# Two gated products per head group moved from VectorE to GpSimd, and earlier writes of a head's reciprocals, in an attention layer

## The chip, the cores and the metric

The kernel runs on one core of one Trainium2 chip. The metric is the device time of one execution in microseconds (us). A core has TensorE (PE in the profile; PEld is its weight load), VectorE (DVE), ScalarE (ACT), GpSimd (POOL) and SyncE (SP). Each engine has its own instruction stream, executed in order; SP and POOL here also issue the DMAs.

## The reference, cut to what matters

The program is a two-layer encoder on 512 tokens with 16 learned meta tokens in front (528 columns), model width 2048: layer 0 is softmax attention, layer 1 gated linear attention. The change lies in layer 0, whose end is

```python
q_blocks = ...                       # 16 heads in 8 groups of 2, one k/v head per group
o = softmax(q k^T / sqrt(128)) v     # per head
return (o * silu(gate)) @ w_out      # gate: a projection as wide as o
```

So each head has a 128 x 528 output `o`, a division by the softmax sums, and a product with `silu(gate)`.

## The kernel before, in words

All matrix products are made in three passes over high and low parts of their operands (`split`: the high part is a copy on ACT, line 131, the low part a subtraction on DVE, line 132). Before the attention groups, gates of heads 0 to 12 are projected and stored in a scratch tensor `g_d` (so "stored gates").

Then one loop goes over `KV` = 8 groups. In group g TensorE does, interleaved: the attention of the two heads of group g, and the projections of k and the two q of group g+1 (`qkv`). After a projection, `rotate` exchanges rows by four DMAs (line 313) and does three products and sums on POOL (lines 314 to 316); line 334 on DVE multiplies by the norm, and the result is split into the next group's q or k.

The attention of a group has nine items: four 128-query tiles of its first head, one item with the 16 meta queries of both heads (index 8), and four tiles of the second head. For each, `softmax` writes scores to the one PSUM tile `s` (TensorE, lines 685 to 687), takes the row maximum `mx` (DVE, line 690), the exponential `pn` (ACT, line 693), and a reciprocal of the sum into a column of `rs` (DVE, line 699). Because `s` has one buffer, the next item's scores can start only when `pn` has been made. Half a slot later `transposed` makes the transposes `pT` (line 705), and their parts `ph` and `pl` (lines 709 and 710), and `weighted` multiplies them by v into `o`, which is copied to `o_sb` (line 730). The first head's `o_sb` is whole soon after item 8.

The outputs are not divided at once. The reciprocals are columns of a small tile and are needed as a row over all partitions, so `inverses` writes them to a scratch tensor `r_d` (SP, lines 645 and 648) and `inverse` reads them back with a broadcast (POOL, line 637). `stored_gates` handles the two heads of the group before: it loads the stored gates into `gr` (POOL, line 654), multiplies by the row norm (DVE, line 658), makes `silu` (ACT, lines 139 to 141; POOL, line 673), calls `inverse`, and then for each head `divided` (POOL, lines 641 and 642) turns `gs` into gate over sum; DVE multiplies `o_sb` by it (line 666), and POOL issues the store to `og_d` (line 667). `gr` and `gs` have two buffers each. Head 13's gate is projected in the last group and handled in the loop itself (line 797).

The order on each engine: the program is written as generators driven by a clock of TensorE's work, where `yield 3.0` says that the next step is to come 3 us later. That gives each instruction its place in the program and with it a priority; weights get a higher one. The compiler's list scheduler then makes each engine's stream by these priorities and by its own estimates of when operands are ready, so an instruction whose operands are expected early can stand well before its place in the program. At run time the streams are fixed, and an instruction that waits holds up all behind it on its engine.

In the stage before, `first_group` normalises group 0's k and q beside the projections. It splits the squares, waits 4.4 us by the clock, and sums them with two matrix products (lines 536 and 537).

Of the kernel before, what the change touches and what calls it, by code (L numbers as in the profile page):

```python
# [14 lines left out]
ALU = mybir.AluOpType  # L15
# [7 lines left out]
SEQ = 512  # L23
META = 16
# [58 lines left out]
def hybrid_encoder(  # L83
# [5 lines left out]
    nc = tc.nc  # L89
    V, A, G, PE = nc.vector, nc.scalar, nc.gpsimd, nc.tensor  # L90
# [12 lines left out]
    og_d = scratch.tile([KT, P, T], F32, name="og_d")  # L103
    h1_d = scratch.tile([4, P, D], F32, name="h1_d")
    g_d = scratch.tile([21, P, T], F32, name="g_d")
    r_d = scratch.tile([KV, 2, T], F32, name="r_d")
# [14 lines left out]
    def col(i):  # L121
        return cols[:, i:i + 1]
# [7 lines left out]
    def split(hi, lo, src):  # L130
        A.copy(hi, src)  # L131
        V.tensor_tensor(lo, src, hi.bitcast(F32), op=ALU.subtract)  # L132

    def rsqrt_inplace(t):
        A.activation(t, t, AF.Ln)
        A.activation(t, t, AF.Exp, scale=-0.5)
# [173 lines left out]
    def rotate(qw, qs):  # L310
        for b in range(4):
            s = b ^ 1
            nc.gpsimd.dma_start(out=qs[b * 32:b * 32 + 32, :], in_=qw[s * 32:s * 32 + 32, :])  # L313
        G.tensor_tensor(qw, qw, cos, op=ALU.mult)
        G.tensor_tensor(qs, qs, sin, op=ALU.mult)
        G.tensor_tensor(qw, qw, qs, op=ALU.add)
# [207 lines left out]
    def first_group():  # L524

        for qw, w in zip(qws, (KN, QN, QN)):
            sq = fr.tile([P, T], F32, tag="sq", name="sq")
            A.activation(sq, qw, AF.Square)
            A.activation(qw, qw, AF.Copy, scale=col(w))
            for a, b in HALVES:  # L530
                parts = fr.tile([P, 2, HALF], F32R, tag="qs", name="shl")
                sh, sl = parts[:, 0], parts[:, 1]
                split(sh, sl, sq[:, a:b])
                yield 4.4
                ps = ps_t.tile([P, 512], F32, tag="t", name="ssq")[:, :HALF]
                PE.matmul(ps, ones_r, sh, start=True, stop=False)
                PE.matmul(ps, ones_r, sl, start=False, stop=True)
                V.scalar_tensor_tensor(sq[:, a:b], ps, 1.0 / P, erow[:, a:b], op0=ALU.mult, op1=ALU.add)
                yield 0.2
            rotate(qw, fr.tile([P, T], F32, tag="qs", name="qs"))  # L540
            rsqrt_inplace(sq)
            yield 9.4
            V.tensor_tensor(qw, qw, sq, op=ALU.mult)
            yield 0.4
# [82 lines left out]
    def qkv(g):  # L627
        qk, outs = qks[g % 2]
        vv = values(g)
        for i, c in enumerate((2048 + g * P, 2 * g * P, (2 * g + 1) * P)):  # L630
            qw, sq, evac = take(col(KN if i == 0 else QN))
            project(w_in0, c, HALVES, evac)
            rope(qw, sq, outs[i], (4.0, 8.8, 9.8))
        return qk, vv

    def inverse(h, rb):
        nc.gpsimd.dma_start(out=rb, in_=r_d[h // 2, h % 2:h % 2 + 1, :].broadcast_to([P, T]))

    def divided(gs, rb):
        by = gs[:, :SEQ].rearrange("p (t q) -> p t q", t=4)  # L640
        G.tensor_tensor(by, by, rb[:, :SEQ].rearrange("p (q t) -> p t q", t=4), op=ALU.mult)
        G.tensor_tensor(gs[:, SEQ:], gs[:, SEQ:], rb[:, SEQ:], op=ALU.mult)

    def inverses(g, rs):
        nc.sync.dma_start(out=r_d[g, :, :SEQ].rearrange("a (p t) -> p a t", t=4),
                          in_=rs[:, :8].rearrange("p (a t) -> p a t", a=2))
        for a in range(2):
            nc.sync.dma_start(out=r_d[g, a, SEQ:].unsqueeze(1), in_=rs[a * META:(a + 1) * META, 8:9])

    def stored_gates(hs, held):  # L650

        grs = [wa.tile([P, T], F32, tag="gr", name="gr") for _ in hs]
        for gr, h in zip(grs, hs):
            nc.gpsimd.dma_start(out=gr, in_=g_d[h])
        yield 8.0
        gss = []
        for gr, h in zip(grs, hs):
            V.tensor_tensor(gr, gr, rrow, op=ALU.mult)
            gss.append(silu(gr))
            inverse(h, gr)  # L660
            yield 5.0
        for gr, gs, h in zip(grs, gss, hs):
            divided(gs, gr)
            yield 3.0
            og = held[h % 2]
            V.tensor_tensor(og, og, gs, op=ALU.mult)
            nc.gpsimd.dma_start(out=og_d[h], in_=og)
            yield 2.0

    def silu(gr):  # L670
        gs = wa.tile([P, T], F32, tag="gs", name="gs", bufs=2)
        sigmoid(gs, gr)
        G.tensor_tensor(gs, gs, gr, op=ALU.mult)
        return gs

    def gate(h, last_k=None):
        gr = wa.tile([P, T], F32, tag="gr", name="gr", bufs=2)
        project(w_in0, 4096 + h * P, HALVES,
                lambda ps, a, b: V.tensor_tensor(gr[:, a:b], ps, rrow[:, a:b], op=ALU.mult), last_k)
        return silu(gr)  # L680
# [33 lines left out]
    def p_tiles():  # L714
        ph = wa.tile([P, 4, 272], F32R, tag="ph", name="ph")
        pl = wa.tile([P, 4, 272], F32R, tag="pl", name="pl")
        pmt = wa.tile([REP, 272], F32R, tag="pmt", name="pmt")
        return ph, pl, pmt
# [18 lines left out]
    def attention(g, qk, vv, o_sb, slot):  # L737
        qh, ql, kh, kl = qk
        q0 = (0, Q1)
        last = g == KV - 1  # L740
        rs = None if last else wa.tile([P, 9], F32, tag="rs", name="rs")
        early, late = [[[None], [None]] for _ in range(2)]

        def tile_of(a, t):
            cell, end = (late, 272) if t > 1 else (early, 256)
            t2 = t % 2
            done = t2 and not (t > 1 and a == 0)
            return (P, q0[a] + t * P, [(cell[a], 0, t2 * P, P)], [(cell[a], 256 * (t > 1), end, a)] if done else [],
                    [] if t2 else [cell[a]], a * 4 + t)
        todo = [tile_of(0, t) for t in range(4)]  # L750
        todo.append((2 * META, SEQ, [(late[a], a * META, 256, META) for a in range(2)], [(late[0], 256, 272, 0)],
                     [late[1]], 8))
        first = tile_of(1, 2)
        todo += [first[:4] + ([],) + first[5:], tile_of(1, 3), tile_of(1, 0), tile_of(1, 1)]
        prev = None
        for item in todo + [None]:
            if item is not None:
                n, c, puts, ends, fresh, i = item
                pn = softmax(n, qh[:, c:c + n], ql[:, c:c + n], kh, kl, None if last else rs[:, i:i + 1])
            yield slot / 2  # L760
            if prev is not None:
                n_, _, puts_, ends_, fresh_, _ = prev[0]
                for cell in fresh_:
                    cell[0] = p_tiles()
                transposed(prev[1], n_, [(cell[0], qc, cc, m) for cell, qc, cc, m in puts_])
                for cell, cc, m, a in ends_:
                    clk.after(slot * 1.1, lambda cell=cell, cc=cc, m=m, a=a:
                              weighted(cell[0], cc, m, vv, o_sb[a], last))
            yield slot / 2
            prev = (item, pn) if item is not None else None  # L770
        if not last:
            inverses(g, rs)
        yield slot * 0.65 if last else 0.0

    def o_tiles():
        return [wa.tile([P, T], F32, tag="o", name="o_sb", bufs=4) for _ in range(2)]

    qk, vv = qks[0][0], values(0)
    held = None
    for g in range(KV):  # L780
        o_sb = o_tiles()
        if g == KV - 1:
            clk.after(10.5, make_sel)
        att = clk.drive(chain(iter([3.0]), attention(g, qk, vv, o_sb, SLOTS[g])))
        gates = [] if g == 0 else [2 * g - 2, 2 * g - 1]
        stored = clk.drive(stored_gates([h for h in gates if h < 13], held))
        if g + 1 < KV:
            nxt = qkv(g + 1)
        for h in gates:
            if h < 13:  # L790
                continue
            gs = gate(h)
            rb = wa.tile([P, T], F32, tag="gr", name="rb")
            inverse(h, rb)
            divided(gs, rb)
            og = held[h % 2]
            V.tensor_tensor(og, og, gs, op=ALU.mult)
            nc.gpsimd.dma_start(out=og_d[h], in_=og)
        if g + 1 < KV:
            clk.finish(att, stored)  # L800
            qk, vv = nxt
            held = o_sb
# [266 lines left out]
    for a, b in HALVES:  # L1069
        ps = ps_t.tile([P, 512], F32, tag="t", name="lrf")[:64, :b - a]  # L1070
        PE.matmul(ps, fold, lt[:, a:b], start=True, stop=True)
        for d in range(2):
            pd, t = ps[d * 32:d * 32 + 16], lrs[d]
# [83 lines left out]
    gs = cg.tile([P, 4, SEQ], F32, name="gs")  # L1157
# [395 lines left out]
```

## Time and profile before

| | |
|---|---|
| median of 3 runs | 1807.34 us (1804.43 to 1808.29) |
| profiled execution, its own time | 1808.31 us |
| its span (first to last instruction) | 1806.5 us |
| mean granted TensorE clock | 0.993 of full |
| attention groups | about 286 to 790 us of the span |
| PE busy | 1750.5 us (97%) |
| DVE busy | 1148.5 us (64%) |
| ACT busy | 1005.5 us (56%) |
| POOL busy | 361.8 us (20%) |

Times in rows are us from the start of the span. A row of the timeline gives start, duration, engine, line, operation and tiles; in brackets stand the engine's idle time just before it and what ended it. A row of the waits gives who waited for whom, the total in us, how often, and the longest. In rows of stretches "PEclk" is the granted TensorE clock as a share of full speed.

### The profile page before, as it was taken

To read this page: it belongs to the slowest core of one execution; us is meant where nothing else is said; L and a number is where in the kernel's file an instruction comes from. 1 tells how busy PE (TensorE), PEld (TensorE's weight loads), DVE (VectorE), ACT (ScalarE), POOL (GpSimd) and SP (SyncE) were. 2 spreads that over 40 slices of the span, in tenths; PEclk is the share of its full clock that TensorE was granted. 3 is DMA by queue.
4 is the path that set the end of the run, shared out by engine and by line. 5 is a ranking of instruction groups with operands and counts; after the bars stand their busy time and mean duration, and the time that the engine had idled before them with its cause. 6 is when DMAs were issued, how large, how long until landed. Compare 5 with 4: busy or idle time off the path is not lost. (4 is left out here: it accounts for less than half of the span.)

```text
span 1806.5 us, 31569 instructions
## 1 busy us (share of the span) xinstructions
PE 1750.5 (97%) x12427; PEld 1641.0 (91%) x12427; DVE 1148.5 (64%) x1805; ACT 1005.5 (56%) x2056; POOL 361.8 (20%) x478
## 2 busy tenths in 40 slices
PE   8999999999999899899999999999999999999998
PEld 8999999998998889899999999988898988888886
DVE  5868765565556555596758776658585865764224
ACT  5635446566656655564547545468585765853221
POOL 3114102434543442232232101110010100000000
PEclk9999999999999999899999999999999999999999
DMA  8444434324322433264476444343342332354323
GB/s 257 141 123 125 131 116 124 96 80 116 103 84 80 111 99 104 71 214 124 130 221 190 121 134 126 95 124 102 86 113 75 114 92 76 99 157 175 94 93 128
DMA packets 272276, 218.81 MB, mean 121 GB/s; under 512 B 13084, under 2 KB 243168, under 8 KB 271600
## 3 DMA queue, kind: packets, MB, share of 16 engines
q1 hardware_dynamic: 253088, 157.41, 30.7%
q0 software_dynamic: 19040, 59.40, 10.0%
q8 instruction: 97, 1.59, 0.4%
q14 instruction: 51, 0.42, 0.1%
HBM read 176.83 MB, written 33.44 MB: 116 GB/s over the span
## 5 line engine op out<-in xcount | busy, mean ns | idle before, releaser
L154 PE MATMUL pp<-uh,whi 128*128 128x264 f32 (+1 forms) x1872 | 587.1, 314 | 1.1 <-POOL whi L383 1.0
L156 PE MATMUL pp<-uh,wlo 128*128 128x264 f32 (+1 forms) x1872 | 577.5, 309 | 1.5 <-DVE wlo L132 1.2
L155 PE MATMUL pp<-ul,whi 128*128 128x264 f32 (+1 forms) x1872 | 578.1, 309 | 0.8 <-DVE ul L445 0.8
L132 DVE TENSOR_TENSOR wlo<-wraw,whi 128x1024 fp32r<-128x1024 f32 (+1 forms) x226 | 275.9, 1222 | 236.3 <-ACT whi L131 231.5
L131 ACT CAST whi<-wraw 128x1024 fp32r<-128x1024 f32 (+1 forms) x226 | 235.2, 1041 | 258.3 <-PE f L1465 83.4
L156 PEld LDWEIGHTS pp<-uh,wlo 128*128 128x128 f32 x1872 | 355.1, 190 | 18.9 <-DVE wlo L132 1.6
L154 PEld LDWEIGHTS pp<-uh,whi 128*128 128x128 f32 x1872 | 355.4, 190 | 17.3 <-POOL whi L383 1.3
L155 PEld LDWEIGHTS pp<-ul,whi 128*128 128x128 f32 x1872 | 355.8, 190 | 14.6 <-DVE ul L445 1.3
L131 ACT CAST whi<-x 128x1024 fp32r<-128x1024 f32 x72 | 75.6, 1050 | 111.6 <-PE pp L241 51.7
L132 DVE TENSOR_TENSOR wlo<-x,whi 128x1024 fp32r<-128x1024 f32 x72 | 93.4, 1302 | 41.7 <-ACT whi L131 41.5
L693 ACT ACTIVATE pn<-s,mx 128x528 f32<-128x528 f32 (+1 forms) x72 | 50.2, 698 | 62.5 <-DVE mx L690 62.4
L240 PE MATMUL px<-uh,whi 128*128 128x264 f32 x288 | 82.2, 285 | 1.2 <-ACT whi L131 1.2
L242 PE MATMUL px<-uh,wlo 128*128 128x264 f32 x288 | 82.1, 285 | 1.0 <-DVE wlo L132 1.0
L241 PE MATMUL px<-ul,whi 128*128 128x264 f32 x288 | 81.5, 283 | 0.0
L1465 PE MATMUL f<-whi,ul 128*128 128x512 f32 x192 | 75.6, 394 | 0.0
L1463 PE MATMUL f<-whi,uh 128*128 128x512 f32 x192 | 75.5, 393 | 0.0
L1464 PE MATMUL f<-wlo,uh 128*128 128x512 f32 x192 | 75.3, 392 | 0.0
L313 POOL DMA_DIRECT2D qs<-qw x96 | 48.1, 506 | 108.1 <-ACT sq L307 70.4
L690 DVE TENSOR_REDUCE mx<-s 128x1 f32<-128x528 f32 (+1 forms) x72 | 50.7, 704 | 29.0 <-PE s L687 28.4
L710 DVE TENSOR_TENSOR pl<-pT,ph 128x512 fp32r<-128x512 f32 (+1 forms) x80 | 47.7, 596 | 25.6 <-ACT ph L709 25.0
L685 PE MATMUL s<-kh,qh 128*128 128x264 f32 (+1 forms) x144 | 43.5, 302 | 19.2 <-ACT pn L693 19.2
L242 PE MATMUL pp<-t0h,wlo 128*128 128x264 f32 x192 | 54.5, 284 | 1.2 <-DVE wlo L132 1.2
(488 smaller groups left out, 4429.7 us busy)
## 6 DMA issues: line engine op xcount, KB each, us to landing
wraw<-in_gla_w_in_dram SPq DMA_DIRECT2D x82, 512.0 KB, 3.9
wraw<-in_attn_w_in_dram SPq DMA_DIRECT2D x75, 512.0 KB, 4.3
wraw<-in_gla_w_out_dram SPq DMA_DIRECT2D x32, 512.0 KB, 3.9
wraw<-in_attn_w_out_dram SPq DMA_DIRECT2D x23, 512.0 KB, 4.4
x<-in_attn_w_in_dram SPq DMA_DIRECT2D x19, 512.0 KB, 4.1
x<-in_gla_w_in_dram SPq DMA_DIRECT2D x14, 512.0 KB, 4.8
qs<-qw POOLq DMA_DIRECT2D x96, 66.0 KB, 4.4
g_d<-y POOLq DMA_DIRECT2D x20, 264.0 KB, 2.4
```

Source lines behind the costliest of these rows:

```text
L131: A.copy(hi, src)
L132: V.tensor_tensor(lo, src, hi.bitcast(F32), op=ALU.subtract)
L154: PE.matmul(ps, wh, uh[:, k, a:b], start=first, stop=False)
L155: PE.matmul(ps, wh, ul[:, k, a:b], start=False, stop=False)
L156: PE.matmul(ps, wl, uh[:, k, a:b], start=False, stop=last)
L240: PE.matmul(ps, w[0][:, k], bh[:, k], start=k == 0 and not more, stop=False, skip_group_check=more)
L241: PE.matmul(ps, w[0][:, k], bl[:, k], start=False, stop=False, skip_group_check=more)
L242: PE.matmul(ps, w[1][:, k], bh[:, k], start=False, stop=k == KH - 1, skip_group_check=more)
L690: V.reduce_max(mx, s, axis=AX.XY, negate=True)
L1463: PE.matmul(ps, uh[:, k, ts], wh[:, kk], start=(k == 0), stop=False)
L1464: PE.matmul(ps, uh[:, k, ts], wl[:, kk], start=False, stop=False)
L1465: PE.matmul(ps, ul[:, k, ts], wh[:, kk], start=False, stop=(k == KT - 1))
```

## The change

Three edits, all in layer 0.

1. In `first_group` the pause between the splits and the sums is 5.6 instead of 4.4 us.
2. `inverses` writes one head at a time. The first head's reciprocals are written in mid group, once item 8's softmax has been issued; the second head's at the end, half a slot earlier than before. A head takes two DMAs on SP; a group took three before and takes four now.
3. The product of `o_sb` with the divided gate is on POOL, directly behind the division, and its store directly behind it, for the 13 stored gates and for head 13.

```diff
@@ first_group
                 split(sh, sl, sq[:, a:b])
-                yield 4.4
+                yield 5.6
@@
-    def inverses(g, rs):
-        nc.sync.dma_start(out=r_d[g, :, :SEQ].rearrange("a (p t) -> p a t", t=4),
-                          in_=rs[:, :8].rearrange("p (a t) -> p a t", a=2))
-        for a in range(2):
-            nc.sync.dma_start(out=r_d[g, a, SEQ:].unsqueeze(1), in_=rs[a * META:(a + 1) * META, 8:9])
+    def inverses(g, rs, a):
+        nc.sync.dma_start(out=r_d[g, a, :SEQ].rearrange("(p t) -> p t", t=4), in_=rs[:, a * 4:a * 4 + 4])
+        nc.sync.dma_start(out=r_d[g, a, SEQ:].unsqueeze(1), in_=rs[a * META:(a + 1) * META, 8:9])
@@ stored_gates
             divided(gs, gr)
+            og = held[h % 2]
+            G.tensor_tensor(og, og, gs, op=ALU.mult)
+            nc.gpsimd.dma_start(out=og_d[h], in_=og)
             yield 3.0
-            og = held[h % 2]
-            V.tensor_tensor(og, og, gs, op=ALU.mult)
-            nc.gpsimd.dma_start(out=og_d[h], in_=og)
-            yield 2.0
@@ attention
             yield slot / 2
+            if not last and (item is None or item[5] == 8):
+                inverses(g, rs, item is None)
             if prev is not None:
...
             prev = (item, pn) if item is not None else None
-        if not last:
-            inverses(g, rs)
@@ the loop over groups, head 13
-            V.tensor_tensor(og, og, gs, op=ALU.mult)
+            G.tensor_tensor(og, og, gs, op=ALU.mult)
```

## The prediction

> **What bounds the kernel now.** I began with the stretches of the span, to see where TensorE is idle.
>
> ```profile
> span 1806.5 us, 31569 instructions
> 286.00:790.00 504.00, 472.19 (x3743) 459.01 (x3743) 297.89 (x569) 308.08 (x750) 200.34 (x245) 0.98 0.36 101
> 790.00:1807.00 1017.00, 1000.57 (x6464) 908.16 (x6463) 648.65 (x1001) 557.46 (x1087) 108.32 (x157) 1.00 0.42 124
> ```
>
> The first number after the length is PE's busy time. TensorE is the bound throughout, but in the attention stage it is idle for 504.0 - 472.2 = 31.8 us, twice as long as in the thousand us behind it, and its granted clock (the third number from the end) is 0.98 there. DVE works for 298 of 504 us there, so it is not full. Next, the waits of PE and of DVE in that stage:
>
> ```profile
> PE s L685 <- ACT pn L693: 19.2, 8, 3.7
> PE pT L705 <- DVE pl L710: 4.3, 5, 1.7
> PE sums L733 <- DVE pl L710: 2.0, 1, 2.0
> ...
> DVE o_sb L666 <- POOL gs L642: 45.8, 13, 7.5
> DVE gr L658 <- DMA gr<-g_d: 15.6, 13, 1.9
> DVE o_sb L797 <- POOL gs L642: 2.2, 1, 2.2
> ```
>
> 19.2 us of PE's idle time are scores that wait for the exponential. The timeline of group 1's start, then of groups 4, 6 and 7, shows what makes it late:
>
> ```profile
> 349.92 0.71 DVE L666 TENSOR_TENSOR o_sb<-o_sb,gs 128x528 f32<-128x528 f32 x1 [2.97 <-POOL gs L642]
> 353.25 1.50 DVE L658 TENSOR_TENSOR gr<-gr,rrow 128x528 f32<-128x528 f32 x1 [0.97 <-DMA gr<-g_d]
> 357.82 0.71 DVE L666 TENSOR_TENSOR o_sb<-o_sb,gs 128x528 f32<-128x528 f32 x1 [2.73 <-POOL gs L642]
> 358.44 0.70 DVE L690 TENSOR_REDUCE mx<-s 128x1 f32<-128x528 f32 x1
> 359.18 0.70 ACT L693 ACTIVATE pn<-s,mx 128x528 f32<-128x528 f32 x1 [1.56 <-DVE mx L690]
> 360.02 0.59 PE L685 MATMUL s<-kh,qh 128*128 128x264 f32 x1 [2.04 <-ACT pn L693]
> 361.21 0.71 DVE L658 TENSOR_TENSOR gr<-gr,rrow 128x528 f32<-128x528 f32 x1 [1.46 <-DMA gr<-g_d]
> ...
> 535.96 0.71 DVE L666 TENSOR_TENSOR o_sb<-o_sb,gs 128x528 f32<-128x528 f32 x1 [5.42 <-POOL gs L642]
> 538.16 0.39 PE L685 MATMUL s<-kh,qh 128*128 128x264 f32 x1 [1.55 <-ACT pn L693]
> 668.71 0.39 PE L685 MATMUL s<-kh,qh 128*128 128x264 f32 x1 [3.01 <-ACT pn L693]
> 723.96 0.71 DVE L666 TENSOR_TENSOR o_sb<-o_sb,gs 128x528 f32<-128x528 f32 x1 [7.50 <-POOL gs L642]
> 726.16 0.59 PE L685 MATMUL s<-kh,qh 128*128 128x264 f32 x1 [3.73 <-ACT pn L693]
> 729.58 0.71 DVE L334 TENSOR_TENSOR qw<-qw,sq 128x528 f32<-128x528 f32 x1 [2.60 <-POOL qw L316]
> ```
>
> The gated product stands in DVE's stream in front of a row maximum and waits for POOL's division; maximum, exponential and the next scores follow one behind the other, and TensorE stops. The pairs at 536 and 724 give the slack: 5.42 - 1.55 = 3.9 and 7.50 - 3.73 = 3.8. A single wait of DVE below about 3.8 us costs TensorE nothing (the one at 349.92 left no gap); a second wait in the same slot costs nearly all of itself (2.73 gave 2.04).
>
> The stretches after five of these stops, of which the first and the last two are shown with the sum of all, have a second price:
>
> ```profile
> 360.40:363.30 2.90, 2.90 (x15) 2.90 (x15) 2.08 (x4) 2.87 (x8) 0.57 (x1) 0.50 0.27 109
> ...
> 726.20:731.00 4.80, 4.80 (x22) 4.80 (x23) 2.13 (x6) 2.13 (x6) 3.80 (x4) 0.50 0.16 54
> 745.50:749.00 3.50, 3.50 (x18) 3.50 (x17) 1.53 (x4) 1.52 (x5) 0.00 (x0) 0.51 0.00 0
> sum 17.50, PE 17.48 PEld 17.48 DVE 10.07 ACT 12.73 POOL 5.98; mean PE 3.50 PEld 3.50 DVE 2.01 ACT 2.55 POOL 1.20
> ```
>
> For 17.5 us in all TensorE had a clock of 0.50 to 0.53: about 17.5 x 0.49 = 8.6 us lost.
>
> **The change, part by part.** The base is the profiled execution's 1808.3 us (span 1806.5 and 1.8 around it), 1.0 above the median.
>
> *Product to POOL.* The nearest rows for its parts:
>
> ```profile
> L666 DVE TENSOR_TENSOR o_sb<-o_sb,gs x13: 707/709/710, 349.9 to 724.0; 128x528 f32<-128x528 f32 x13
> L673 POOL TENSOR_TENSOR gs<-gs,gr x16: 1316/1323/1336, 298.7 to 780.9; 128x528 f32<-128x528 f32 x16
> L667 POOL DMA_DIRECT2D og_d<-o_sb x13: 547/587/590, 354.1 to 725.0; - x13
> ```
>
> DVE loses 14 x 0.71 = 9.9 us of work and, what counts, the 45.8 + 2.2 us in which it waited for POOL. POOL gains 14 x 1.32 = 18.5 us; it is busy for 200 of 504. In its own stream the product needs no signal from another engine beyond `o_sb`, and the store follows it as it did. What goes from the path: the scores' waits 19.2, the transposes' waits 4.3 (each follows a slot that DVE began late), the `sums` wait 2.0 (DVE's `pl` stood behind head 13's product), and the half clock 8.6: 34.1 us.
>
> *What DVE waits for next.* It no longer stops for POOL's lateness, so it meets it at line 658, whose gate load (POOL, line 654) is issued only when the division has freed `gr`. Of these 13 waits 11 come behind a division. At a group's start the lateness is the 2.97 + 0.97 = 3.9 us of the first two rows of the timeline, and up to 1.32 + 0.59 = 1.9 more if the product and its store are issued ahead of the load. Against a slack of 3.8 this is 0.1 to 2.0 us of TensorE each, 1 to 22 in all. I take 0.4, near the lower end, since that pair of waits, the nearest row, left no gap and the second pair, which cost 2.04, goes to another place: 11 x 0.4 = +4.4.
>
> *Reciprocals in mid group.* Rows of group 0:
>
> ```profile
> 316.54 0.79 SPq L648 DMA_DIRECT2D r_d<-rs  x2
> 339.55 0.57 SPq L645 DMA_DIRECT2D r_d<-rs  x1
> 325.42 2.01 POOL L313 DMA_DIRECT2D qs<-qw  x4 [9.45 <-ACT sq L307]
> 329.56 0.39 ACT L730 COPY o_sb<-o 128x272 f32<-128x272 f32 x1 [0.87 <-PE o L728]
> 333.25 1.33 POOL L316 TENSOR_TENSOR qw<-qw,qs 128x528 f32<-128x528 f32 x1
> 341.11 0.71 DVE L334 TENSOR_TENSOR qw<-qw,sq 128x528 f32<-128x528 f32 x1 [0.43 <-issue]
> 343.53 0.59 POOL L637 DMA_DIRECT2D gr<-r_d  x1 [8.95 <-DMA r_d<-rs]
> 348.17 1.54 POOL L641 TENSOR_TENSOR gs<-gs,gr 128x512 f32<-128x512 f32 x1 [1.52 <-DMA gr<-r_d]
> ```
>
> Both small writes already leave at item 8, because their operands are ready; now the first head's large one can leave with them at about 316.5. With the 4.0 us from 339.55 to 343.53 and the 4.6 from there to 348.17, its division comes at about 325 instead of behind the boundary, and its product after the copy at 329.56. So one of the two chains that collide at each boundary moves to a quieter place: this is why I expect one wait per slot and not two. On SP there are seven more DMAs of under 0.6 us, 4 us at most; they stand where line 648 stood, wait for no later reciprocal, and only weight loads are behind them: 0. On POOL the rotation is behind the division and product: 1.76 + 1.32 + 0.59 = 3.7 us later in mid group, covered because line 316 ends at 334.6 and line 334 starts at 341.1, 6.5 later; without that cover it would be the excess over 6.5. At the boundary the last rotation gets 1.9 us more in front but loses one broadcast and one division: 0, with +1 as upper bound each (7 in all).
>
> *POOL against DVE.* The row at 353.25 took 1.50 us, the same work at 361.21 took 0.71: the first ran beside a product of POOL. A product on POOL can then hold a DVE product of two SBUF operands by 0.8 us; 14 of them are 0 to 11 us of DVE, within the slack: 0.
> [...]
>
> *The pause of 5.6.* The rows of the earlier stage:
>
> ```profile
> PE ssq L537 <- DVE shl L132: 1.2, 2, 0.6
> L537 PE MATMUL ssq<-shl,ones_r x6: 279/283/391, 122.2 to 172.6; 128*128 128x264 f32 x6
> ```
>
> A gain of 0 to 1.2; the six pauses push the chain out by 7.2 us, and after 172.6 there are over 100 us of cover until 286. I take 0, as the wait may pass to another row.
>
> **Sum:** 1808.3 - 34.1 + 4.4 = 1778.6, say 1779.
>
> **The rivals.**
> (a) *The wait moves to line 658.* If product and store stand before the gate load, the upper bound above holds: +22 instead of +4.4, so 1796. For it: POOL's stream puts what is first in the program first. Against: the load needs only the division's end.
> (b) *The early write brings nothing*, because the first head's chain still runs at the boundary. Then two waits per slot stay and about half the 34.1 goes: 1791. Against: both small writes did leave at 316.54.
> (c) *Slower: POOL's rotation becomes the bound.* Line 334 would wait for line 316, with the next group's q and the row maximum behind it. To undo 34.1 us, each of seven boundaries must cost 4.9, so the rotation must be late by 3.8 + 4.9 = 8.7 us; at 10 us the time is 1808.3 - 34.1 + 7 x 6.2 = 1818. For it: at the last boundary line 334 waited 2.6 for POOL. Against: only 3.7 us are put in front of it.
> (d) *The half clock is not due to these stops*, apart from the longest. Then 12.7 x 0.49 = 6.2 us stay: 1785. Against: five stretches, each right behind a stop of about 2 us or more; for it: a stop of 3.0 at 668.7 had none.
> [...]
> (e) *POOL holds DVE* for the whole 11 us on the path: 1790.
>
> **How the numbers follow.** Main case 0.55 (own range 1773 to 1788), (a) 0.18, (b) 0.09, (c) 0.06, (d) 0.05, (e) 0.04, nothing measurable (a pile-up of several of these terms) 0.03. The lower end is the 34.1 with no new wait and the pause's gain, and some us for other DVE work that comes earlier: 1770; the upper end takes in (a), (b), (e) and some room: 1801. 0.2% (3.6 us) is about what a measurement of this kernel tells from no change: faster 0.88, same 0.05, slower 0.07.
>
> **What would show it.** Right: line 666 is gone from DVE's waits and nothing of 45 us takes its place; the scores' wait for `pn` is under 6 us; no stretch at half clock in the groups; line 637 and the first division of each group lie in mid group. Wrong: DVE's wait at line 658 grows from 15.6 beyond 40 us (a), or line 334 waits for POOL by more than 3.8 us at each boundary (c), or the clock stays at 0.98 in the stage although the stops are gone (d).

## The result, and the profile after

The changed kernel takes 1799.52 us (median of 5 runs, 1796.92 to 1800.92) against 1808.29 for the kernel before, a ratio of 0.9953 (95%: 0.9939 to 0.9968). It is 8.8 us faster where 29 were forecast. Its profiled execution took 1799.52 us too.

In the changed kernel the lines behind the edit have moved up by two or three: the row norm is line 656 (it was 658), the gate load 652 (654), the gated product on POOL 663 and its store 664 (666 and 667), the row maximum 687 (690), the exponential 690 (693), the scores 682 (685), the transposes 702 (705), `pl` 707 (710).

Span, and two stretches (as before: PE's busy time is the number after the length, its clock the third from the end); the second stretch is the only one at half clock behind a stop in the attention groups:

```profile
span 1797.5 us, 31585 instructions
286.00:790.00 504.00, 478.82 (x3855) 465.55 (x3854) 308.63 (x573) 315.82 (x757) 227.37 (x262) 1.00 0.40 108
364.50:367.10 2.60, 2.60 (x14) 2.60 (x13) 2.54 (x6) 1.66 (x5) 0.00 (x0) 0.51 0.12 28
```

PE is idle for 504.0 - 478.8 = 25.2 us of the same 504, where it was 31.8, and the clock is 1.00 instead of 0.98. The waits in that window show what was exchanged:

```profile
PE s L682 <- ACT pn L690: 12.8, 6, 3.0
PE pT L702 <- DVE pl L707: 6.0, 12, 0.7
...
DVE gr L656 <- DMA gr<-g_d: 28.9, 9, 5.3
DVE qw L334 <- POOL qw L316: 7.7, 2, 4.8
```

DVE's 45.8 us at the product are gone, and the wait for the gate load has grown from 15.6 to 28.9. The scores still wait for 12.8 us where 19.2 stood, now once at each of six boundaries. Where the stage begins and ends is told by its groups of scores and of output casts, here after (first and last start stand behind the three durations):

```profile
L682 PE MATMUL s<-kh,qh x144: 280/284/422, 293.1 to 755.3; 128*128 128x264 f32 x128, 128*32 128x264 f32 x16
L131 ACT CAST uh<-o_sb x2: 636/642/647, 771.1 to 774.9; 128x528 fp32r<-128x528 f32 x2
```

Before, the first scores started at 290.5 and the last cast of an output at 786.6. From the one to the other the stage takes 481.8 us instead of 496.1: 14.3 gained. Ahead of it 2.6 are lost (290.5 to 293.1), and behind it 2.7. The program behind it is unchanged, and in the seventeen profiles of this study that part took 1019.6 to 1023.3 us (1026.2 in one), so this loss is not put down to the change. The sum, -14.3 + 2.6 + 2.7 = -9.0, is the difference of the spans.

The timeline of the changed kernel: the first rows are the early write, the mid-group division and the next gate's row norm in group 0, then come the boundary to group 1, the boundary at 541 on DVE, ACT and PE, and the end of the last of six boundaries with a stop.

```profile
312.10 0.34 SPq L645 DMA_DIRECT2D r_d<-rs  x1
324.18 1.56 POOL L641 TENSOR_TENSOR gs<-gs,gr 128x512 f32<-128x512 f32 x1 [3.14 <-DMA gr<-r_d]
330.38 0.69 DVE L656 TENSOR_TENSOR gr<-gr,rrow 128x528 f32<-128x528 f32 x1
...
341.89 0.57 SPq L645 DMA_DIRECT2D r_d<-rs  x1
345.61 0.58 POOL L637 DMA_DIRECT2D gr<-r_d  x1 [5.72 <-DMA r_d<-rs]
350.92 1.54 POOL L641 TENSOR_TENSOR gs<-gs,gr 128x512 f32<-128x512 f32 x1 [2.49 <-DMA gr<-r_d]
352.72 1.32 POOL L663 TENSOR_TENSOR o_sb<-o_sb,gs 128x528 f32<-128x528 f32 x1
353.99 0.59 POOL L652 DMA_DIRECT2D gr<-g_d  x1
354.57 0.55 POOL L664 DMA_DIRECT2D og_d<-o_sb  x1
358.20 1.51 DVE L656 TENSOR_TENSOR gr<-gr,rrow 128x528 f32<-128x528 f32 x1 [4.96 <-DMA gr<-g_d]
363.31 0.39 PE L682 MATMUL s<-kh,qh 128*128 128x264 f32 x1 [3.00 <-ACT pn L690]
...
541.55 0.93 DVE L656 TENSOR_TENSOR gr<-gr,rrow 128x528 f32<-128x528 f32 x1 [5.33 <-DMA gr<-g_d]
542.57 0.65 ACT L139 ACTIVATE gs<-gr 128x528 f32<-128x528 f32 x1 [4.78 <-DVE gr L656]
542.75 0.69 DVE L687 TENSOR_REDUCE mx<-s 128x1 f32<-128x528 f32 x1
543.12 0.63 ACT L135 ACTIVATE sq<-sq 128x528 f32<-128x528 f32 x1
543.65 0.63 ACT L140 ACTIVATE gs<-gs 128x528 f32<-128x528 f32 x1
544.19 0.63 ACT L136 ACTIVATE sq<-sq 128x528 f32<-128x528 f32 x1
544.72 0.63 ACT L141 ACTIVATE gs<-gs 128x528 f32<-128x528 f32 x1
545.25 0.68 ACT L690 ACTIVATE pn<-s,mx 128x528 f32<-128x528 f32 x1
546.08 0.39 PE L682 MATMUL s<-kh,qh 128*128 128x264 f32 x1 [2.84 <-ACT pn L690]
...
664.20 0.71 DVE L334 TENSOR_TENSOR qw<-qw,sq 128x528 f32<-128x528 f32 x1 [4.82 <-POOL qw L316]
666.40 0.39 PE L682 MATMUL s<-kh,qh 128*128 128x264 f32 x1 [1.50 <-ACT pn L690]
```

The first head of group 0 went as forecast: its division comes at 324.18, and the gate loaded into the freed buffer (330.38) costs DVE no wait. At the boundary the second head's reciprocals leave at 341.89, come back as a broadcast that POOL can use at 350.92, 9.0 us later, and behind division and product, but ahead of the product's store, the gate load is issued at 353.99. DVE waits 4.96 us for it, then TensorE 3.00.

The boundary at 541 shows why the slack was not 3.8. The row maximum ends at 542.75 + 0.69 = 543.44, and the exponential starts only at 545.25: on ACT five activations stand in front of it, three of the silu that the waiting gate has just released (139 to 141) and two of the next group's norm (135 and 136). In the kernel before, the same step went from 359.14 to 359.18. The same five stand there at each of the five boundaries where DVE waits for the load. DVE's wait and TensorE's stop were 4.96 and 3.00, 4.30 and 1.66, 5.06 and 2.43, 5.33 and 2.84, 3.98 and 1.40: a slack of 2.5 to 2.6, and of 2.0 at the first boundary, where the row norm itself took 1.51. The lateness was forecast at 3.9 us and up to 1.9 more; it came to between 4.0 and 5.3. At the last of the six stops, DVE waits for POOL's rotation (664.20) instead, at 1.50 of TensorE.

### The profile page after: what moved, and what is told of

Same layout as the page of the kernel before. It is cut to its first block, busy times and chain, and to the rows that moved or that the text cites. A ratio compares the mean times of both kernels' runs of the same rounds, so it can differ in the third digit from the quotient of the medians.

```text
span 1797.5 us, 31585 instructions
## 1 busy us (share of the span) xinstructions
PE 1746.3 (97%) x12427; PEld 1636.9 (91%) x12427; DVE 1141.4 (63%) x1791; ACT 1005.9 (56%) x2056; POOL 383.2 (21%) x492
## 5 line engine op out<-in xcount | busy, mean ns | idle before, releaser
L240 PE MATMUL pp<-t0h,whi 128*128 128x264 f32 x192 | 55.6, 289 | 3.7 <-ACT y L270 3.7
L240 PEld LDWEIGHTS px<-uh,whi 128*128 128x128 f32 x288 | 54.7, 190 | 2.1 <-ACT whi L131 2.1
```

The costliest lines, as they stand in the source:

```text
L240: PE.matmul(ps, w[0][:, k], bh[:, k], start=k == 0 and not more, stop=False, skip_group_check=more)
```

## The experiments

My theory was that the six stops are the second head's reciprocals' trip through `r_d`, handed on through POOL's stream to the gate load. Unless said otherwise, the kernels below are the changed one with the pause set back to 4.4, so that the stage ahead is that of the kernel before; their base is then the first of them. Ratios are to the kernel before, on the same chip.

### What each part of the change does

The pause alone set back:

```
-                yield 5.6
+                yield 4.4
```

> The changed kernel with the pause in first_group back at 4.4. If the pause is what made the stage before attention longer (first scores at 293.1 us instead of 290.5, with a DVE product that waits 3.88 us for POOL's rotation), the first scores return to about 290.5 and the time falls from 1799.5 by 2 to 3 us, to about 1797. If the delay came from the other two edits, it stays at 1799.5.

1794.97 us, 0.9931 (0.9913 to 0.9950). The first scores start at 290.6 instead of 293.1 (in all fourteen profiles with 4.4 at 290.4 to 292.8, in the three with 5.6 at 292.9 to 295.4), but the stage ends at 775.0 as with the pause of 5.6 (774.9).

The kernel before with the pause alone:

```
-                yield 4.4
+                yield 5.6
```

> The kernel before with the pause of 5.6 alone. By the theory that the pause costs by itself: slower by 2 to 3 us, about 1811. By the rival that it costs only together with the other edits: within 1 us of before.

1809.03 us, 1.0012 (1.0000 to 1.0025). Its first scores start at 292.9. The waits show where the 2.4 come from, in this kernel ahead of the attention:

```profile
PE pp L240 <- ACT y L270: 3.5, 2, 3.0
```

Six sums written later in the program let other work go first, and a projection's wait for ACT of up to 3.0 us takes the place of the 1.2 that the pause saved. The changed kernel has the same wait. In time it is between nothing and about 0.2% (1.0012 here, and 0.9931 beside 0.9953, with intervals that overlap), and these runs don't settle it.

Products on POOL, with the reciprocals written at the group's end as before:

```
         divided(gs, gr)
-        yield 3.0
         og = held[h % 2]
-        V.tensor_tensor(og, og, gs, op=ALU.mult)
+        G.tensor_tensor(og, og, gs, op=ALU.mult)
         nc.gpsimd.dma_start(out=og_d[h], in_=og)
-        yield 2.0
+        yield 3.0
...
```

> The kernel before with the gated products on POOL behind their division, and nothing else: the reciprocals are written at the group's end and the pause is 4.4. Theory: DVE no longer waits for the division but still for the gate loads behind it, for both heads at the boundary, so the scores' waits stay above 12 us; gain 3 to 8 us, about 1802. Rival (the products on DVE were the whole trouble): the scores' waits fall below 5 us and the time to below 1790.

1822.91 us, 1.0082 (1.0063 to 1.0102): slower, where theory and rival both expected a gain. The stage, its waits and one boundary:

```profile
286.00:790.00 504.00, 463.15 (x3619) 452.30 (x3619) 280.58 (x537) 298.26 (x733) 214.59 (x251) 0.96 0.34 94
PE pT L704 <- DVE pl L709: 20.3, 4, 5.7
PE s L684 <- ACT pn L692: 18.0, 6, 4.8
...
427.17 0.71 DVE L658 TENSOR_TENSOR gr<-gr,rrow 128x528 f32<-128x528 f32 x1 [4.90 <-DMA gr<-g_d]
430.36 1.12 PE L704 MATMUL pT<-ident,pn 128*128 128x128 f32 x4 [5.51 <-DVE pl L709]
```

With both divisions at the boundary the product (422.36 to 423.70) delays the gate load, DVE waits for that 4.90 us, and the low part `pl` behind it stops the transposes for 5.51. DVE's 45.8 us at the product are gone and its waits for the load grow from 15.6 to 37.3; in sum it waits less than before, but in longer stops at the row norm, and TensorE is idle for 504.0 - 463.2 = 40.9 us of the stretch instead of 31.8. The granted clock falls from 0.98 to 0.96 besides, by estimate 504 x 0.02 = 10 us. The two longest waits of the scores, 4.83 and 4.84, come behind row norms that waited 5.30 and 5.01 us for the load and then took 3.54 and 3.79 us instead of 0.71, beside POOL's products.

The early reciprocals alone, in the kernel before:

```
-    def inverses(g, rs):
+    def inverses(g, rs, a):
...
             yield slot / 2
+            if not last and (item is None or item[5] == 8):
+                inverses(g, rs, item is None)
...
-        if not last:
-            inverses(g, rs)
```

> The kernel before with the first head's reciprocals written in mid group, and nothing else: products on DVE, pause 4.4. Theory: one chain per boundary instead of two brings most of what was gained, 8 to 12 us, about 1798, with one wait of DVE for POOL left per half group. Rival (the move to POOL brings the gain): within 3 us of before.

1799.47 us, 0.9959 (0.9946 to 0.9972): as much as the whole change.

```profile
PE s L683 <- ACT pn L691: 10.2, 10, 1.6
...
DVE o_sb L664 <- POOL gs L642: 22.1, 6, 4.6
```

DVE still waits for POOL, 22.1 us at six products, but only once per group (its waits for the gate load stay at 15.2), and the stops become short (1.6 at most). The changed kernel run once more beside it:

> The changed kernel as it is, on the chip of this call, so that the next kernels (all with the pause of 4.4) can be set beside it. It was 0.9953 of before. If the pause costs 4 us, as 0.9931 without it suggests, it stays near 0.995 here while kernels without the pause lie lower.

1797.68 us, 0.9950 (0.9929 to 0.9971). The move to POOL therefore costs 0.8% without the early write and makes no clear difference with it: 0.9953 and 0.9950 beside 0.9959, and at the same pause 0.9931, whose interval just overlaps that of 0.9959, so a gain of some 0.3% is not excluded. The early write is worth 0.4% with the products on DVE and 1.5% with them on POOL (1.0082 to 0.9931). In this second profile of the changed kernel the scores wait for 10.1 us instead of 12.8, and two stretches run at half clock instead of one, so a difference of 2 or 3 us between two profiles says little.

### Is it the trip, the buffers, or the place of the load?

The trip taken away: the broadcast row is read from a scratch tensor that was written long before, so the kernel leaves out the division by the sums.

```
-        nc.gpsimd.dma_start(out=rb, in_=r_d[h // 2, h % 2:h % 2 + 1, :].broadcast_to([P, T]))
+        nc.gpsimd.dma_start(out=rb, in_=g_d[h % 8, 0:1, :].broadcast_to([P, T]))
```

> The changed kernel, pause 4.4, with one source changed: the row that the division multiplies by is read from a tensor stored long before, in place of the reciprocals (the attention's division is left out in effect). So a division no longer waits for the trip of the reciprocals through DRAM; all instructions stay. Theory (lateness of that trip reaches the gate load behind the division and from there DVE at line 656): DVE's wait for gate loads falls from 27.5 to under 10, the scores' waits from 13.4 to under 4, time about 1784. Rival (POOL's load itself, or its hold on DVE's operands, is what delays DVE): the scores' waits stay above 10 and the time near 1795.

1849.97 us, 1.0237 (1.0214 to 1.0259). The scores' waits are gone, as the theory says, but transposes wait instead, the granted clock of the stage is 0.93, and the time is 55 us over its base.

```profile
571.63 0.58 POOL L652 DMA_DIRECT2D gr<-g_d  x1 [0.31 <-POOL gs L642]
574.85 0.71 DVE L656 TENSOR_TENSOR gr<-gr,rrow 128x528 f32<-128x528 f32 x1 [10.46 <-DMA gr<-g_d]
576.22 1.11 PE L702 MATMUL pT<-ident,pn 128*128 128x128 f32 x4 [9.11 <-DVE pl L707]
```

DVE now waits 10.46 us for a gate load that POOL issues only 3.2 us before the end of that wait, right behind the division: the row norm stands some 7 us too early in DVE's stream. The likely reason is the list scheduler, which expects a division without a trip to free its buffer early; that is argued from the order of the streams, not measured. The theory in its first form fell. The trip sets when the load comes, but how long DVE waits is set by how far ahead of that the row norm stands.

More buffers, so that the load doesn't have to wait for a division (`o_sb` gives up one of its own for room):

```
-        grs = [wa.tile([P, T], F32, tag="gr", name="gr") for _ in hs]
+        grs = [wa.tile([P, T], F32, tag="gr", name="gr", bufs=4) for _ in hs]
...
-        return [wa.tile([P, T], F32, tag="o", name="o_sb", bufs=4) for _ in range(2)]
+        return [wa.tile([P, T], F32, tag="o", name="o_sb", bufs=3) for _ in range(2)]
...
```

> The changed kernel, pause 4.4, with four buffers for gr instead of two (and three instead of four for o_sb, to make room), two for gs as before. The gate load needs no division now, so DVE's wait at line 656 should all but vanish. Theory that any engine which meets the late chain passes the wait on: ACT's line 139 then waits for the gs buffer that POOL's product frees, and the scores' waits stay at 8 to 14, time 1790 to 1796. Rival (only the wait on DVE matters): scores' waits under 4, time about 1784.

1809.25 us, 1.0012 (0.9998 to 1.0026): the whole gain is lost.

```profile
DVE gr L656 <- DMA gr<-g_d: 6.4, 7, 3.1
ACT gs L139 <- POOL o_sb L663: 30.2, 11, 6.4
...
355.48 3.41 DVE L656 TENSOR_TENSOR gr<-gr,rrow 128x528 f32<-128x528 f32 x1 [0.49 <-DMA gr<-g_d]
362.88 0.39 PE L682 MATMUL s<-kh,qh 128*128 128x264 f32 x1 [2.85 <-ACT pn L690]
```

DVE's wait falls from 27.5 to 6.4 and ACT takes it over: the silu needs a `gs` buffer, which POOL's product frees, and the exponential stands behind it. That is only part of the 18.4 us for which the scores wait here. Three more stops, of 2.85, 2.81 and 2.80, come behind row norms that hardly waited but took 3.4 us, beside two products of POOL in a row (355.71 to 358.31 at the first). Three of each of the three tiles instead:

```
-        grs = [wa.tile([P, T], F32, tag="gr", name="gr") for _ in hs]
+        grs = [wa.tile([P, T], F32, tag="gr", name="gr", bufs=3) for _ in hs]
...
-        gs = wa.tile([P, T], F32, tag="gs", name="gs", bufs=2)
+        gs = wa.tile([P, T], F32, tag="gs", name="gs", bufs=3)
...
-        return [wa.tile([P, T], F32, tag="o", name="o_sb", bufs=4) for _ in range(2)]
+        return [wa.tile([P, T], F32, tag="o", name="o_sb", bufs=3) for _ in range(2)]
...
```

> The changed kernel, pause 4.4, with three buffers each for gr and gs (and three for o_sb). A gate is now prepared half a group ahead of the division that used to free its buffers, so neither DVE nor ACT meets the late chain. Theory: the scores' waits fall under 4 us, DVE's wait at line 656 under 10, time about 1784. Rival (POOL's load at the boundary delays the rotation, line 334 or the clock whatever the buffers): above 1792.

1793.47 us, 0.9925 (0.9903 to 0.9946), the base's 0.9931. DVE's wait for the load is 28.3 us where the base has 27.5. The load still leaves behind the boundary's division (at 473.47, with the division at 470.41), and DVE waits for it 5.15 us there.

The load held back: a one-column copy that needs the first head's `o_sb` stands ahead of each gate load.

```
         for gr, h in zip(grs, hs):
+            G.tensor_copy(gr[:, :1], held[0][:, :1])
             nc.gpsimd.dma_start(out=gr, in_=g_d[h])
```

> The changed kernel, pause 4.4, with one column of the group's first o_sb copied into gr (POOL, 128x1) ahead of each gate load, which then overwrites it. The copy holds the load, and with it line 656 and the silu, until the group's first output is there, about 27 us into the group, where no division stands just in front. Behind a division then stand only the product and its store, on POOL. Theory (DVE and ACT are delayed because gate loads stand behind divisions): DVE's wait for gate loads falls below 15 us, the scores' waits from about 13 to under 4, the stage runs at full clock, time about 1782. Rival (POOL's boundary itself, with its rotation and its hold on DVE's operands, delays DVE): the scores' waits stay above 8 and the time above 1792.

1822.36 us, 1.0081 (1.0059 to 1.0103).

```profile
380.08 0.31 POOL L652 COPY gr<-o_sb 128x1 f32<-128x1 f32 x2
383.70 0.71 DVE L657 TENSOR_TENSOR gr<-gr,rrow 128x528 f32<-128x528 f32 x1 [4.40 <-DMA gr<-g_d]
...
425.80 0.71 DVE L334 TENSOR_TENSOR qw<-qw,sq 128x528 f32<-128x528 f32 x1 [4.50 <-POOL qw L316]
```

The loads left the boundary, but for a place behind POOL's rotation in mid group (380.08), where DVE waits 4.40 us for them as well; and the rotation at the boundary is late now (425.80). The same copy in the other three combinations, first with the early reciprocals and DVE's products:

> The same column copy, with early reciprocals, but the products on DVE as before (pause 4.4). Theory: DVE waits for a division once per half group, about 3 us each, under the slack of 3.8 us and with no silu behind it, so the scores' waits are under 6 us; time 1783 to 1790, at most 6 us above the one with products on POOL. If the products on DVE were the trouble that the prediction saw, it is 10 us or more above it.

1822.97 us, 1.0082 (1.0055 to 1.0109). With POOL's products and the late reciprocals:

> The same column copy, products on POOL, but the reciprocals of both heads written at the group's end (pause 4.4). Without the copy this was 1823. Theory (what hurt there was gate loads behind two divisions, not POOL's own queue): the transposes' waits of 20 us vanish, time 1785 to 1798; what is left is line 334 waiting for a rotation behind two divisions. Rival (POOL's queue at the boundary is too long by itself): above 1810.

1827.7 us, 1.0112 (1.0090 to 1.0135). In the kernel before:

> The kernel before with the column copy alone: products on DVE, reciprocals of both heads at the group's end, pause 4.4. DVE still stops for two divisions at each boundary. Theory: the gate loads' share of the waits goes, the products' share stays; scores' waits 8 to 16 us instead of 19, time 1794 to 1804.

1841.74 us, 1.0187 (1.0162 to 1.0212). The scores' waits in the four are 19.7, 15.8, 29.3 and 36.4 us, so none of the four theories held. Three kernels were made slower by the copy, by 1.2 to 1.9%; for the one with POOL's products and late reciprocals the intervals overlap (1.0112 beside 1.0082). With the copy, the early reciprocals are worth 1.05% on DVE's products and 0.3% on POOL's, and the move to POOL 0.75% with late reciprocals (1.0187 to 1.0112) and nothing with early ones (1.0082 to 1.0081): here either part alone brings most of what both bring. Without the copy it is different, since there the move alone costs time. In neither case do the parts add up.

### Taking the lateness itself away

Odd heads without gate work (load, norm, silu and division; their product takes the row of norms):

```
+        even = [h for h in hs if h % 2 == 0]
...
-            G.tensor_tensor(og, og, gs, op=ALU.mult)
+            G.tensor_tensor(og, og, rrow if h % 2 else gs, op=ALU.mult)
```

> The changed kernel, pause 4.4, without the gate load, row norm, silu and division of the odd heads 1 to 11 (their product on POOL is kept, by another row). So nothing of a gate stands at a group's boundary; the even heads' chain in mid group stays. Theory (what is left of the scores' waits comes from gate work behind the odd head's late division, and the prices of the forecast were right): scores' waits from about 13 to under 3 us, no stretch at half clock, time about 1780, less some 2 us for work left out. Rival (the waits come from rotation and row maximum at the boundary whatever the gates do): scores' waits above 8, time above 1788.

1775.66 us, 0.9819 (0.9805 to 0.9832).

```profile
286.00:750.00 464.00, 453.68 (x3683) 443.10 (x3683) 285.68 (x541) 297.77 (x729) 195.21 (x222) 1.00 0.36 100
PE pT L705 <- DVE pl L710: 4.0, 7, 1.1
```

No scores wait for an exponential, TensorE's largest item of waits is 4.0 us over seven transposes, and its idle time is 464.0 - 453.7 = 10.3 us. A time near the forecast's 1779 comes once the second head's gate work is off the boundary. The run takes away more than lateness, though: the odd heads' work on DVE, ACT and POOL, and the second user of the two `gr` buffers. How the 19 us to the base divide among these it does not show.

The trip made shorter: the broadcast read is issued by SP instead of POOL.

```
-        nc.gpsimd.dma_start(out=rb, in_=r_d[h // 2, h % 2:h % 2 + 1, :].broadcast_to([P, T]))
+        nc.sync.dma_start(out=rb, in_=r_d[h // 2, h % 2:h % 2 + 1, :].broadcast_to([P, T]))
```

> The changed kernel, pause 4.4, with the broadcast read of the reciprocals issued by SP, right behind their write, in place of POOL. POOL is no longer held at line 637 and the read starts as soon as the write has landed. Theory (the boundary is late by the real length of the trips): the wait of POOL's division for its row shrinks from 33 us, DVE's wait for gate loads by 5 to 10, the scores' waits to 4 to 10, time 1787 to 1793. Rival: SP now stops for the write to land and weight loads behind it come late, or nothing changes: 1795 or more.

1789.4 us, 0.9885 (0.9867 to 0.9903): the fastest kernel that computes everything, 0.46% under its base and 0.7% under the change by the ratios.

```profile
PE s L682 <- ACT pn L690: 4.4, 5, 1.8
...
342.02 0.53 SPq L645 DMA_DIRECT2D r_d<-rs  x1
345.53 0.34 SPq L637 DMA_DIRECT2D gr<-r_d  x1
349.19 1.54 POOL L641 TENSOR_TENSOR gs<-gs,gr 128x512 f32<-128x512 f32 x1 [0.64 <-DMA gr<-r_d]
```

From the write to the division it is 7.2 us where the base has 8.8 at this boundary, and over the six boundaries it is shorter by 0.2 to 1.7 us, 1.2 on average. DVE's wait falls from 27.5 to 17.8, and the scores' wait from 13.4 to 4.4. At the third, fourth and fifth boundaries the trip is shorter by 1.29, 1.30 and 1.28 us and TensorE's stop by 1.25, 1.26 and 1.25: what the trip loses, the stop loses. At the first two, where the trip is 1.7 shorter, the stops of 2.79 and 1.73 are gone; at the sixth, where DVE waits for the rotation, trip and stop lose 0.2 each. Why the read is quicker from SP is open: in the base POOL stood idle for the write to land before it issued the read (in the changed kernel for 5.72 us, the row at 345.61), so no product held it there.

Last, the copy ahead of the odd heads' loads only, on the last column, so that they stay near their place:

```
+            if h % 2:
+                G.tensor_copy(gr[:, :1], held[0][:, SEQ - 1:SEQ])
             nc.gpsimd.dma_start(out=gr, in_=g_d[h])
```

> The changed kernel, pause 4.4, with the column copy ahead of the gate loads of odd heads alone, from the last columns of the group's first o_sb, which is whole in mid group behind the first rotation. In the kernel with copies ahead of both loads two silus met POOL's late rotation in mid group; here each head's gate has its own place, and no gate load stands behind the boundary's division. Theory: scores' waits 4 to 10, DVE's wait for gate loads under 20, line 334 waits for POOL at each boundary by 2 to 5 us, time 1785 to 1800. Rival (as with both copies, any work moved to mid group collides there): above 1805.

1812.49 us, 1.0023 (1.0009 to 1.0037).

```profile
PE pT L704 <- DVE pl L709: 11.2, 16, 1.3
```

The scores' waits fall to 2.1 us, but transposes and outputs (5.8 us for line 724) wait instead, and there is no gain over the kernel before. Of the things tried, holding the load back moved the lateness, more buffers did not help, and a shorter trip or no gate work at the boundary took the stops down. Taking the trip away altogether did not, since DVE's stream then met the load far too early.

## Why the prediction was right or wrong

**The sum's largest term**, the scores' 19.2 us taken off the path, was mis-sized: 12.8 remain. The wait of DVE at line 666 went as forecast, but "What DVE waits for next" is the step that failed. It named the place (the gate load), the product and store ahead of the load, and an upper bound (22, rival (a)), and then took 0.4 us per wait, near the lower end. Both numbers behind that choice were off. Its 0.4 stands for waits of 4.2; at five boundaries they were 4.0 to 5.3, since the product, though not its store, did stand ahead of the load. And the slack was 2.0 to 2.6 instead of 3.8, since it had been read where a product of DVE was followed by a maximum, while a waiting row norm releases the silu, whose activations go ahead of the exponential on ACT. A slack holds for the instruction that waited when it was measured, not for the next one. Five stops behind the load cost 11.3 us, 2.3 each, where 11 of 0.4 were booked; the sixth, of 1.5, is behind POOL's rotation, which the sum had at nothing. Rival (a)'s 1796 is within 4 us of what came, but partly by luck: it counted 11 stops of 2.0 and no waits of transposes, and its own sign, more than 40 us at the load, did not come (28.9).

**The transposes' 4.3** did not go; 6.0 us of such waits stand there, short ones (0.7 at most). They are 5.9 with the shorter trip and 4.0 without the odd heads' gates, where the scores' stops are small or gone, so they do not just follow slots that DVE began late, as the forecast had it; what makes them is open. **The sums' 2.0** is no longer among TensorE's waits; with the early write alone, which leaves head 13's product on DVE, it still is. **The half clock** went for the most part: one stretch of 2.6 us at 0.51 is left, by estimate 2.6 x 0.49 = 1.3 us lost, against 8.6. In the second profile of the same kernel two stretches of 3.5 us at 0.53 and 0.52 are left, about 3.3 lost. This speaks against rival (d), which had 6.2 staying, but does not settle what brings such a stretch on: most of the stops that remain are followed by none.

In the stage, -29.7 was forecast and -14.3 measured; the 15.4 between are the scores' 12.8, the transposes' 6.0 and the clock's 1.3, less the 4.4 that had been booked, which makes 15.7.

**Reciprocals in mid group** moved as forecast, and this part carries the gain: alone it gives 0.9959. That the division was forecast at 325 and came at 324.18 is luck: the write left at 312.10 instead of 316.5, and from there it took 12.1 us instead of 8.6. Rival (b) is refuted. That the products on POOL were needed to collect it is refuted too. The forecast treated the POOL move as the part that frees DVE and the early write as its helper; the runs show the early write halving DVE's waits for POOL by itself (45.8 at 13 products to 22.1 at six), and the move passing the rest on to the load.

**The pause** was costed at nothing "as the wait may pass to another row". It did, and the first scores start 2.6 us later; the stage ends at the same time, and a cost in the total of up to about 0.2% stays open.

**Rivals (c) and (e).** The rotation was late twice (7.7 us in all), where (c) needed it at every boundary; the column copy in the changed kernel brought (c) in part, with seven waits of DVE for the rotation, 29.8 us in all, and the time at 1822. As to (e), POOL held DVE's row norm for 0.8 us at the first boundary and for at most 0.2 at the other four, which is inside the 12.8. No run takes this hold away alone, and in the kernels with POOL's products alone and with four `gr` buffers it came to 2.6 to 3.1 us at a time.

## What to carry to other kernels

When an in-order engine stops waiting for a late producer, list everything else that it takes from that producer (a buffer, a load issued behind it, a rotation), and charge the lateness to the next of them with the slack of that instruction, counting what it releases on other engines ahead of the critical one. Here moving the consumer onto the late engine did not shorten the chain (1.0082 alone); moving the chain's start earlier (0.9959 alone), or making its trip shorter (0.46% under its base), did. Seven writes moved by half a group were worth 0.4%, the product's change of engine nothing clear beside it. The two edits that touch the same chain did not add, and one of them cost time without the other, so each should be timed alone and both together.

## What the runs showed of the hardware

- Some DVE products took far longer beside products of POOL. In the changed kernel the same DVE product took 0.71 us at 343.45 and 1.87 at 324.43, beside POOL's division of 324.18; a row norm took 0.69 at 391.95 and 1.80 at 454.36, beside POOL's product of 454.27. With four `gr` buffers a row norm took 3.41 us (355.48 to 358.89) beside two products of POOL in a row, which ended at 358.31:

```profile
324.43 1.87 DVE L334 TENSOR_TENSOR qw<-qw,sq 128x528 f32<-128x528 f32 x1 [0.83 <-ACT sq L136]
```

- In these runs the half clock was not a matter of one stop's length. A stop of 2.04 us in the kernel before was followed by a clock of 0.50, one of 3.00 in the changed kernel by 0.51, and the one of 2.84 at 546.08 by none below 1.00. In the second profile of the changed kernel the stop at that boundary (3.06) was followed by 0.52. In the last experiment no wait of TensorE in the groups was over 1.5 us, and still there were four such stretches. Before the first of them TensorE was busy for only 1.75 of 3.70 us, in several short stops:

```profile
408.50:412.20 3.70, 1.75 (x11) 1.13 (x9) 3.64 (x4) 2.42 (x6) 3.70 (x6) 1.00 0.17 41
412.50:415.50 3.00, 3.00 (x16) 3.00 (x16) 0.92 (x3) 0.22 (x1) 0.49 (x2) 0.50 0.86 186
```

- Two short DMAs through a scratch tensor cost far more here than their own issue, which took 0.57 us for the write at 341.89 and 0.58 for the read at 345.61: from the write's issue on SP to the first use of the row by POOL 8.9 to 10.2 us at the six boundaries of the changed kernel, and 7.2 to 9.2 when SP issues the read as well.
